# Input projections of a delta-rule stage taken by pairs of channel tiles in seven block products, with operands parked in DRAM

## The chip, the cores and the metric

One core of one Trainium2 chip runs the whole kernel. The metric is device microseconds of one execution, the median of several runs. TensorE multiplies, VectorE, ScalarE and GpSimd work elementwise, and the SyncE queue issues all DMAs.

## What is computed

One decoder block over x of 1024 tokens by 1024 features, in float32. Cut to what matters here:

```python
proj = x @ w_in                       # columns: q k v z beta a | sparse attention | merge gates
q, k, v = silu(causal_dwconv4(q|k|v)) # 4 heads of 128, taps along the tokens
o_A  = chunk_gated_delta(l2norm(q), l2norm(k), v, g, beta)   # chunks of 64 tokens
o_A  = rmsnorm(o_A) * silu(z)
o_B  = native_sparse_attention(...)   # compressed, selected and window branches
m    = sigmoid(gA) * (o_A @ W_A) + sigmoid(gB) * (o_B @ W_B)
h    = LayerNorm(alpha * x + m @ W_out)
out  = LayerNorm(alpha * h + (silu(c_g) * c_v) @ W_down)     # [c_g|c_v] = dwconv3(h @ W_up)
```

## The kernel before

Products are made in three matmuls: each operand is split into a rounded part (`h`) and its residue (`l`), and `h*h`, `h*l`, `l*h` are added up. A weight tile of 1024 x 128 is loaded (`load_cols`, L186), rounded on ScalarE and its residue taken on GpSimd (`split`, L180 to L184). x is kept transposed in four SBUF blocks `xT` (rounded and residue, two halves of 512 tokens), from the pool `S6` of six buffers of 2 MB; the other two hold `vS` (attention values) and `gA` (gates and output of the delta rule).

The head (L244 to L273): for each of eight token tiles, `turn_x` transposes x on TensorE, ScalarE and VectorE write the two parts, and `v_group` makes the attention values with 24 matmuls of 288 columns. Behind it small constants are prepared: masks, `chan_cols` and `pos_cols` (L308 to L334; taps and position vectors, loaded into `st`, which has two buffers, and transposed), the decays `gg` and their running sums `gc`.

The delta-rule stage (L426 to L705) makes 33 projections, each `proj_gen` (L415): 48 matmuls of 512 columns into a two-bank PSUM tile `big` (two of them) and then a `use`: `act_gen` (convolution and silu of q, k, v, 12 tiles), `z_gen` (4), `mix_gen` (merge gates, 16 tiles, stored to DRAM) and, at the end, one key projection of the attention. `PLAN` (L39) says which are made in which of nine units. Into their matmuls two generators are woven for each of 4 heads x 2 halves: `pre` (L477: norms, decay matrices, inversion of the unit lower triangular matrix, its 16 x 16 blocks by a loop of small VectorE operations L534 to L550 with DRAM images in between) and `scan` (L616: the state recurrence over four pairs of chunks). `PRE` and `SCAN` (L35, L36) say at which part of a unit each step of theirs is issued. TensorE's order is the order in which the program issues (`manual_schedule`, for TensorE alone); the other engines and SyncE are ordered by the scheduler of the language. PSUM has eight banks: two `big` of two, and four `sm` of one.

After the stage the attention, the merge and the feed-forward part follow. The feed-forward products of `W_up` are made in seven block products already, in an order that a planner of the kernel works out.

Of the kernel before, what the change touches and what calls it, by code (L numbers as in the profile page):

```python
# [16 lines left out]
OP = mybir.AluOpType  # L17
# [21 lines left out]
def PLAN(z, M, QKV, F):  # L39
    return [[F(z, 1)] + M(3), QKV(1) + M(1), [F(z, 2)] + M(2), QKV(2) + M(1),  # L40
            [F(z, 3)] + M(2), QKV(3), M(3), M(3), M(1)]
# [105 lines left out]
def hybrid_block_kernel(ctx: ExitStack, tc: tile.TileContext, x, w_in, gdn_conv_w, gdn_a_log,  # L147
# [16 lines left out]
    psb = ps_cm.enter_context(tc.tile_pool(name="psb", bufs=2, space=bass.MemoryType.PSUM))  # L164
    pss = ps_cm.enter_context(tc.tile_pool(name="pss", bufs=4, space=bass.MemoryType.PSUM))
    dram = ctx.enter_context(tc.tile_pool(name="dram", bufs=1, space=bass.MemoryType.DRAM))

    def big():
        return psb.tile([128, 1024], F32, name="big", tag="big")

# [29 lines left out]
    xT = {}  # L200
    for hf in range(2):
        for p in "hl":
            xT[p, hf] = S6.tile([128, KT, 512], F32R, name=f"xT{p}{hf}", tag="s")
# [9 lines left out]
    ones = const.tile([128, 128], F32, name="ones")  # L213
    V.memset(ones, 1.0)
# [8 lines left out]
    sp = gmask.tile([128, NT, 32], F32, name="sp")  # L223
# [17 lines left out]
    for tt in range(2, NT):  # L241
        load_x(tt)

    def turn_x(tt):  # L244
        ps = big()
        for k in range(KT):
# [3 lines left out]
        A.activation(xT["h", hf][:, :, o:o + 128], psv, AF.Copy)  # L250
        V.tensor_tensor(xT["l", hf][:, :, o:o + 128], psv,
                        xT["h", hf][:, :, o:o + 128].bitcast(F32), op=OP.subtract)
# [14 lines left out]

    with tc.manual_schedule(engines=MS):
        turn_x(0)
        for tt in range(NT):  # L270
            if tt + 1 < NT:
                turn_x(tt + 1)
            v_group(tt)  # L273
    triu = gmask.tile([128, 128], F32, name="triu")
# [15 lines left out]
    eye = gmask.tile([32, 16, 16], F32, name="eye")  # L290
    V.memset(eye, 0.0)
    for i in range(16):
        V.memset(eye[:, i, i:i + 1], 1.0)
# [14 lines left out]
    def chan_cols(src, taps, tiles, name):  # L308
        st = xin.tile([128, 1024], F32, name="st", tag="st", bufs=2)[:tiles, :taps * 128].rearrange("p (k c) -> p k c", k=taps)
# [117 lines left out]
    with gd as gp:  # L427
# [49 lines left out]
        def pre(h, hf, st):  # L477
# [108 lines left out]
            for b in (16, 32, 64):  # L586
# [10 lines left out]
                if b < 64:  # L597
                    X = g5("X")
# [1254 lines left out]
```

## Time and profile before

| | us |
|---|---|
| median of 3 runs | 1719.05 (1718.46 to 1721.38) |
| profiled execution, its own time | 1719.78 |
| its span, first to last instruction | 1718.0 |
| TensorE busy | 1675.0 |
| VectorE, GpSimd, ScalarE busy | 1116.2, 788.1, 734.2 |

The page of the profile gives the busy time of each engine and the chain of work that ended last, followed back from the end. The views below it give windows of time, single instructions in order of time, groups of instructions by line, and waits. A TensorE instruction's listed duration includes its pipeline, so its cost in a stream is read from start to start.

### The profile page before, as it was taken

What the parts mean: (1) busy time and instruction counts of PE and PEld (TensorE: products, weight loads), DVE (VectorE), ACT (ScalarE), POOL (GpSimd) and SP (SyncE); (2) the same over time, 40 slices, a digit from 0 to 9 for tenths busy, and PEclk for the clock granted to TensorE, in tenths of its full rate; (3) what the DMA queues carried; (4) which work ended last, traced back from release to release, by engine and by line L of the source; (5) the groups of instructions that cost most, each with busy time, mean ns of one, the idle gap of its engine ahead of it and who ended that gap; (6) DMA issues with size and microseconds to landing.
All of it is one profiled execution on the core that took longest, in us unless ns stands there. A gap on an engine that the chain in (4) does not pass through costs nothing.

```text
span 1718.0 us, 23466 instructions
## 1 busy us (share of the span) xinstructions
PE 1675.0 (97%) x8562; PEld 1411.7 (82%) x8562; DVE 1116.2 (65%) x2089; ACT 734.2 (43%) x1269; POOL 788.1 (46%) x640
## 2 busy tenths in 40 slices
PE   8999999999999998999999999999999999999997
PEld 8888888888888877888877887788888888888885
DVE  3545647657433358899874328988677667865656
ACT  3422323223222458788843115544444444443333
POOL 1322222232212537887657236678877777210005
PEclk9999999999999999999999999999999999999998
DMA  5222121221221312334125612333332232687722
GB/s 177 75 63 76 56 66 45 61 75 33 87 81 52 98 63 96 126 105 132 35 87 184 224 58 89 111 107 116 118 104 93 98 112 98 215 315 269 234 88 98
DMA packets 199024, 189.88 MB, mean 111 GB/s; under 512 B 19656, under 2 KB 155005, under 8 KB 198909
## 3 DMA queue, kind: packets, MB, share of 16 engines
q1 hardware_dynamic: 198909, 188.39, 34.3%
q8 instruction: 67, 1.10, 0.3%
q14 instruction: 48, 0.39, 0.1%
HBM read 136.97 MB, written 51.38 MB: 110 GB/s over the span
## 4 chain that ended last, share of the span: by engine, by line
PE 82%; DVE 7%; issue 3%; ACT 3%; POOL 3%; DMA 2%; SPq 0%; ACTq 0%; POOLq 0%; DVEq 0%
PE pq L193 37%; PE big L193 29%; PE sm L193 12%; PE sm L983 2%; DVE st L917 1%; ACT P L919 1%; POOL P L872 1%; DVE wh L991 1%; DMA w<-in_w_out_dram 1%; DVE wl L991 1%; DVE st L881 0%; DVE wb L1454 0%; DMA w<-in_w_down_dram 0%; DMA wsum<-w 0%; PE big L247 0%
## 5 line engine op out<-in xcount | busy, mean ns | idle before, releaser
L183 POOL TENSOR_TENSOR wl<-w,wh 128x1024 fp32r<-128x1024 f32 (+2 forms) x51 | 123.1, 2418 | 362.1 <-PE big L193 132.9
L193 PE MATMUL big<-xTl,wh 128*128 128x512 f32 x608 | 244.1, 402 | 0.0
L193 PE MATMUL big<-xTh,wh 128*128 128x512 f32 x608 | 244.1, 401 | 0.0
L193 PE MATMUL pq<-wd 128*128 128x512 f32 x924 | 209.6, 389 | 0.0
L193 PEld LDWEIGHTS pq<-wd 128*128 128x128 f32 x924 | 173.4, 188 | 36.0
L193 PE MATMUL pq<-xb,wb 128*128 128x512 f32 x792 | 187.6, 391 | 2.0 <-DVE accs L1465 1.5
L1465 DVE SCALAR_TENSOR_TENSOR accs<-pq,fcw,accs 128x510 f32<-128x510 f32 (+3 forms) x264 | 144.5, 568 | 61.0 <-ACT accs L1553 56.1
L193 PEld LDWEIGHTS pq<-xb,wb 128*128 128x128 f32 x792 | 148.5, 188 | 34.8 <-issue 2.8
L193 PE MATMUL big<-xTh,wl 128*128 128x512 f32 x608 | 160.3, 399 | 0.0
L193 PEld LDWEIGHTS big<-xTl,wh 128*128 128x128 f32 x608 | 114.7, 189 | 20.7 <-issue 0.2
L193 PEld LDWEIGHTS big<-xTh,wh 128*128 128x128 f32 x608 | 114.7, 189 | 20.6
L193 PE MATMUL pq<-mTh,wb 128*128 128x512 f32 x528 | 127.6, 397 | 3.2 <-ACT mTh L1253 3.1
L193 PEld LDWEIGHTS big<-xTh,wl 128*128 128x128 f32 x608 | 110.9, 188 | 21.4
L193 PE MATMUL pq<-mTl,wb 128*128 128x512 f32 x528 | 127.3, 391 | 0.0
L872 POOL TENSOR_TENSOR P<-P,st 128x640 f32<-128x640 f32 (+6 forms) x94 | 106.3, 1160 | 45.1 <-DVE st L881 19.7
L193 PEld LDWEIGHTS pq<-mTh,wb 128*128 128x128 f32 x528 | 101.1, 192 | 25.8 <-ACT mTh L1253 3.3
L193 PEld LDWEIGHTS pq<-mTl,wb 128*128 128x128 f32 x528 | 99.1, 188 | 21.2
L1454 POOL TENSOR_TENSOR wb<-w,wb 128x512 fp32r<-128x512 f32 x79 | 103.7, 1319 | 27.2 <-ACT wb L1253 27.2
L182 ACT ACTIVATE wh<-w 128x1024 fp32r<-128x1024 f32 (+2 forms) x51 | 53.1, 1046 | 134.8 <-PE big L193 90.7
L193 PE MATMUL big<-kS,qS 128*128 128x320 f32 (+5 forms) x384 | 86.7, 343 | 3.2 <-ACT P L919 2.0
L919 ACT ACTIVATE P<-big,st 128x640 f32<-128x640 f32 (+6 forms) x112 | 83.3, 749 | 10.3 <-DVE st L917 9.5
L1253 ACT ACTIVATE wb<-w 128x512 fp32r<-128x512 f32 x85 | 53.3, 629 | 80.3 <-PE pq L193 76.0
(394 smaller groups left out, 3558.1 us busy)
## 6 DMA issues: line engine op xcount, KB each, us to landing
w<-in_w_in_dram SPq DMA_DIRECT2D x40, 512.0 KB, 3.9
w<-in_w_up_dram SPq DMA_DIRECT2D x36, 512.0 KB, 3.8
w<-in_w_down_dram SPq DMA_DIRECT2D x53, 256.0 KB, 3.7
wsum<-w SPq DMA_DIRECT2D x44, 256.0 KB, 2.5
sig<-th SPq DMA_DIRECT2D x32, 256.0 KB, 2.2
w<-sig SPq DMA_DIRECT2D x30, 256.0 KB, 3.3
wx<-in_w_up_dram SPq DMA_DIRECT2D x11, 512.0 KB, 3.8
gdrC<-accs SPq DMA_DIRECT2D x11, 512.0 KB, 2.6
```

The costliest lines, as they stand in the source:

```text
L182: A.activation(wh[:, :n], w[:, :n], AF.Copy)
L183: G.tensor_tensor(wl[:, :n], w[:, :n], wh[:, :n].bitcast(F32), op=OP.subtract)
L193: PE.matmul(o, a, b, start=start, stop=stop, skip_group_check=True)
L872: G.tensor_tensor(p, p, r.to_broadcast([128, p.shape[1]]), op=OP.mult)
L917: V.reduce_max(nm, pv if m > 1 else pv[:, 0], axis=AX.X, negate=True)
L919: A.activation(P[:, r0 + i, :n], pv[:, i], AF.Exp, bias=nm[:, i:i + 1], accum_out=su[:, i:i + 1])
L983: PE.transpose(tp[:n, r * 128:(r + 1) * 128], P[:, r, c0:c0 + n], ident)
L991: V.tensor_tensor(pl, tp[:n], ph.bitcast(F32), op=OP.subtract)
L1253: A.activation(o, i, AF.Copy)
L1454: e.tensor_tensor(H.tile[:, 1], src(), H.tile[:, 0].bitcast(F32), op=OP.subtract)
L1465: V.scalar_tensor_tensor(o, i, fcw[:, 2 - s, j:j + 1], o, op0=OP.mult, op1=OP.add)
```

## The change

The 32 projections of the delta-rule stage are taken by pairs of channel tiles. For a pair, the weights are 2 x 2 blocks (two channel tiles by two halves of the features), x has 2 x 2 blocks (two halves of the features by two halves of the tokens), and the four results come from seven block products of 12 matmuls (the scheme of Strassen and Winograd) with sums of blocks before and after. The sums of x are made once: on GpSimd from the rows of x (`row_sums`), turned on TensorE (`turn_sum`), as blocks 6, 7, 4 and 5. The sums of the weights are made on GpSimd for each pair. The results are combined by VectorE in four PSUM banks of one each (`psbk`, in place of the two `big`), and each `use` is now called by halves of the tokens.

To make room, `vS` and one block of x are stored to DRAM in the head and loaded again at the end of the stage; z and the gated output go to DRAM tiles `zd` and `gAd`, and `gA` is loaded at the end. The row of running decay sums is stored to DRAM (`gcd`) and read back by every `pre` as a broadcast, in place of a product with `triu`. `chan_cols` and `pos_cols` move into the hand-ordered head, behind value group 4. In `pre`, the two scalings of `kt` move from GpSimd to ScalarE, the unit matrix in `XB` is made on GpSimd, and the turn of v comes later; several tiles have fewer buffers. One plan over nine units replaces `PLAN`: one pair is made ahead, then the matmuls of the others are spread evenly.

```diff
-PRE = [0.0, 0.04, 0.07, 0.1, 0.14, 0.2] + [0.72 + 0.05 * i for i in range(8)]
-SCAN = [1.13 + 0.085 * i for i in range(8)] + [1.81, 1.86, 1.92]
+PRE = [0.0, 0.07, 0.1, 0.14, 0.8] + [0.82 + 0.05 * i for i in range(8)]
+SCAN = [1.2 + 0.085 * i for i in range(8)] + [1.88, 1.93, 1.99]
+PAIRS = ["kq0", "vz0", "m", "kq1", "vz1", "m", "kq2", "vz2", "m", "m", "kq3", "vz3", "m", "m", "m", "m"]
+SPAN = 9.0
...
+    XS = {1: XK[0, 0], 2: XK[1, 0], 3: XK[1, 1], 6: xblock("xT2"), 7: xblock("xT3", S7)}
+    def row_sums(tt):
+        (a, b), (c, d) = [[xi[t][:, hs] for hs in HS] for t in (tt - 4, tt)]
+        rows = {5: a, 6: d, 7: c, 4: b}
+        for o, x, y in ((a, c, a), (c, d, c), (d, d, a), (b, d, b)):
+            G.tensor_tensor(o, x, y, op=OP.subtract)
+        return rows
+    def turn_sum(n, tt, row):
+        ps = sm()
+        for k in range(4):
+            PE.transpose(ps[:, k * 128:(k + 1) * 128], row[:, k * 128:(k + 1) * 128], ident)
...
+        A.activation(r[:, 0], psv, AF.Copy)
+        V.tensor_tensor(r[:, 1], psv, r[:, 0].bitcast(F32), op=OP.subtract)
...
             v_group(tt)
+            if tt % 2:
+                nc.sync.dma_start(vsp[:, (tt - 1) * 512:(tt + 1) * 512],
+                                  vS[:, tt - 1:tt + 1].rearrange("p t b s d -> p (t b s d)").bitcast(F32))
+            if tt == 4:
...
+                gcw = chan_cols(gdn_conv_w[0], 4, 12, "gcw")
+                fcw = chan_cols(ffn_conv_w[0], 3, 2 * NFF, "fcw")
+                nrw = chan_cols(gdn_norm_w, 1, 1, "nrw")
...
+                peT = {"k": pos_cols(cmp_pos_k, "pek"), "v": pos_cols(cmp_pos_v, "pev")}
+            if tt >= 4:
+                rows[tt] = row_sums(tt)
+            if tt == NT - 1:
+                nc.sync.dma_start(xsp, XK[0, 1].rearrange("p i k c -> p (i k c)").bitcast(F32))
+            for t in {5: (4,), 6: (5,), 7: (6, 7)}.get(tt, ()):
+                for n in (6, 7):
+                    turn_sum(n, t, rows[t][n])
+        for n, name in ((4, "xT4"), (5, "xT1")):
+            XS[n] = xblock(name)
+            for t in range(4, NT):
+                turn_sum(n, t, rows[t][n])
...
+            gr = g5("tmp", 3)
+            nc.sync.dma_start(gr, bass.AP(tensor=gcd.tensor, offset=gcd.offset + (hf * 16 + h) * 128,
+                                          ap=[[0, 128], [512, 4], [1, 128]]))
             yield
-            gb = g5("tmp", 3)
-            A.activation(gb, gg[:, cs, h, None].to_broadcast([128, 4, 128]), AF.Copy)
-            gr = sm()
-            for c in range(4):
-                mm(gr[:, csl[c]], gb[:, c, :], triu)
             dS = g5("tmp", 3)
...
-            G.tensor_tensor(kb, kt, bc(nb), op=OP.mult)
-            G.tensor_tensor(kd, kd, bc(egd[:, cs, h]), op=OP.mult)
+            for c in range(4):
+                A.activation(kb[:, c], kt[:, c], AF.Copy, scale=nb[:, c:c + 1])
+                A.activation(kd[:, c], kd[:, c], AF.Copy, scale=egd[:, hf * 4 + c, h:h + 1])
...
+        PORD = (1, 6, 2, 7, 5, 4, 3)
+        class Seven:
+            def make(self):
...
+                sub = functools.partial(G.tensor_tensor, op=OP.subtract)
+                if n == 1:
+                    self.load(2 * g + 1)
+                    src = A11
+                elif n == 6:
+                    self.load(2 * g + 2)
+                    G.tensor_tensor(self.s, A21, A22, op=OP.add)
+                    sub(A21, A11, A21)
+                    sub(A11, self.s, A11)
+                    src = A11
...
+                t = self.ring[self.made % 5]
+                A.activation(t[:, :512], src, AF.Copy)
+                sub(t[:, 512:], src, t[:, :512].bitcast(F32))
...
+            def steps(self):
+                u2, u3 = self.uu[:, HS[0]], self.uu[:, HS[1]]
+                for _ in range(4):
+                    self.make()
+                for g, ((_, one), (_, two)) in enumerate(self.pairs):
+                    a, b, c, d = (self.banks[i] for i in ((0, 2, 1, 3) if g % 2 else range(4)))
+                    bank = {1: a, 2: a, 6: b, 4: b, 7: c, 5: d, 3: d}
+                    for n in PORD:
+                        self.make()
...
+                        if n == 1:
+                            A.activation(u2, a, AF.Copy)
+                        elif n == 6:
+                            V.tensor_tensor(u2, b, u2, op=OP.add)
+                        elif n == 7:
+                            V.tensor_tensor(u3, c, u2, op=OP.add)
+                        elif n == 5:
+                            V.tensor_tensor(c, d, u3, op=OP.add)
+                            two(1, c)
+                        elif n == 2:
+                            one(0, a)
+                        elif n == 4:
+                            V.tensor_tensor(b, u3, b, op=OP.subtract)
+                            two(0, b)
+                        else:
+                            V.tensor_tensor(d, d, u2, op=OP.add)
+                            one(1, d)
...
+                XK[0, 1] = xblock("xK01b")
+                nc.sync.dma_start(XK[0, 1].rearrange("p i k c -> p (i k c)").bitcast(F32), xsp)
+                yield from proj_gen(C_KC, kc_ps.append, one_bank)
...
+            fg, done = chain(), 0
+            for _ in range(84):
+                next(fg)
+            for x, _, g in ev:
+                while done < x * (84 * len(PAIRS) - 84 + 48) / SPAN:
+                    next(fg, None)
+                    done += 1
+                next(g, None)
...
+    vS = S6.tile([128, NT, 2, 4, 64], F32R, name="vS", tag="s")
+    nc.sync.dma_start(vS.rearrange("p t b s d -> p (t b s d)").bitcast(F32), vsp)
+    gA = S6.tile([128, 4, T], F32, name="gA", tag="s")
+    for j in range(4):
+        nc.sync.dma_start(gA[:, j], gAd[j])
```

## Rows read from the trace of the kernel before

**Rows 1.** The page: shares of the span by engine in the chain.
```profile
PE 82%; DVE 7%; issue 3%; ACT 3%; POOL 3%; DMA 2%; SPq 0%; ACTq 0%; POOLq 0%; DVEq 0%
```
**Rows 2.** Windows: window, length, busy PE, PEld, DVE, ACT, POOL, granted clock, DMA.
```profile
20.00:40.00 20.00, 20.00 (x160) 20.00 (x159) 8.88 (x16) 7.14 (x11) 0.00 (x0) 1.00 0.30 82
...
1200.00:1300.00 100.00, 100.00 (x440) 82.37 (x439) 69.75 (x115) 43.47 (x72) 80.20 (x62) 1.00 0.32 106
...
44.00:545.00 501.00, 499.89 (x2738) 427.43 (x2738) 274.63 (x740) 143.87 (x240) 127.45 (x76) 1.00 0.23 64
```
**Rows 3.** The chain in order of time: start, length, what, merged.
```profile
534.20 8.49 PE big L193 x37
...
1115.99 590.20 PE pq L193 x2592
```
**Rows 4.** Timeline of TensorE: start, duration, instruction; head, stage start, decay product, end.
```profile
36.66 1.03 PE L247 MATMUL big<-ident,x 128*128 128x128 f32 x8
37.45 0.38 PE L193 MATMUL sm<-wh,xTh 128*128 128x288 f32 x1
...
45.08 0.51 PE L193 MATMUL big<-xTh,wh 128*128 128x512 f32 x1
...
146.59 1.05 PE L193 MATMUL sm<-triu,tmp 128*128 128x128 f32 x8
147.40 0.48 PE L193 MATMUL big<-xTh,wh 128*128 128x512 f32 x1
...
545.95 0.39 PE L193 MATMUL sm<-xTh,wh 128*128 128x512 f32 x1
```
**Rows 5.** Timeline of TensorE behind two idle waits (in brackets, with the releaser).
```profile
684.31 0.62 PE L983 MATMUL sm<-ident,Pc 128*64 128x128 f32 x4 [2.28 <-DVE oB L968]
...
1067.41 9.02 PE L193 MATMUL pq<-mTh,wb 128*128 128x512 f32 x24 [3.09 <-ACT mTh L1253]
```
**Rows 6.** Windows of 4 us behind these waits: busy PE, granted clock, DMA.
```profile
684.00:688.00 4.00, 3.69 (x17) 0.59 0.55 169
...
1068.00:1072.00 4.00, 3.88 (x10) 0.50 0.03 9
```
**Rows 7.** DMA issues: count, size, median us from issue to landing.
```profile
w<-in_w_in_dram SPq DMA_DIRECT2D x40, 512.0 KB, 3.9
...
hres<-h SPq DMA_DIRECT2D x8, 512.0 KB, 2.6
...
AB<-aimg SPq DMA_DIRECT2D x8, 32.0 KB, 1.9
```
**Rows 8.** Groups of instructions by form: count, busy us, mean ns, idle before.
```profile
L1454 POOL TENSOR_TENSOR wb<-w,wb 128x512 fp32r<-128x512 f32 x79 | 103.7, 1319 | 27.2 <-ACT wb L1253 27.2
...
L1614 POOL TENSOR_TENSOR accs<-accs 128x512 f32<-128x512 f32 x13 | 22.1, 1700 | 47.6 <-ACT wd L1701 34.7 <-DVE accs L1614 12.8
...
L389 POOL TENSOR_TENSOR rr<-ss,mhalf 128x4 f32<-128x4 f32 x16 | 16.1, 1008 | 6.9 <-DVE ss L493 6.4
...
L1253 ACT ACTIVATE wb<-w 128x512 fp32r<-128x512 f32 x85 | 53.3, 629 | 80.3 <-PE pq L193 76.0 <-DMA w<-in_w_up_dram 2.6 <-issue 1.0
...
L881 DVE TENSOR_TENSOR st<-st,gates 128x4 f32<-128x4 f32 x48 | 21.3, 443 | 0.9
L1570 DVE TENSOR_TENSOR u<-pq,u 128x512 f32<-128x512 f32 x22 | 15.1, 685 | 0.9 <-PE pq L193 0.2
```
**Rows 9.** Timeline of GpSimd and VectorE in the delta-rule stage.
```profile
187.55 2.38 POOL L183 TENSOR_TENSOR wl<-w,wh 128x1024 fp32r<-128x1024 f32 x1 [11.29 <-ACT tmp L648]
...
187.88 2.08 DVE L651 TENSOR_TENSOR ms<-ms,sc 128x4 f32<-128x4 f32 x1
...
193.19 0.12 DVE L654 TENSOR_TENSOR ms<-ms,rr 128x4 f32<-128x4 f32 x1
```
**Rows 10.** Window of the operations on tile `pr`: busy VectorE.
```profile
60.00:530.00 470.00, 53.86 (x256) 1.00 0.23 65
```
**Rows 11.** Waits: engine, line, waited for, total us, times, longest.
```profile
POOL ms L389 <- DVE ms L652: 30.3, 8, 11.5
```

More of the change, by code (lines that the diff above doesn't have):

```diff
@@ L169, in big, with one_bank @@
         return psb.tile([128, 1024], F32, name="big", tag="big")
+    def one_bank():
+        return psb.tile([128, 512], F32, name="bk", tag="bk")
     def sm():
@@ L198, in hybrid_block_kernel, with xblock, __init__, __getitem__ @@
     V.tensor_copy(identr, ident)
[L200 to L203, printed above, removed]
+    def xblock(name, pool=S6):
+        return pool.tile([128, 2, 4, 512], F32R, name=name, tag="s")
+    XK = {(kh, hf): xblock(f"xK{kh}{hf}") for hf in range(2) for kh in range(2)}
+    class Blocks:
+        def __init__(self, p, hf):
+            self.p, self.hf = "hl".index(p), hf
+        def __getitem__(self, i):
+            return XK[i[1] // 4, self.hf][i[0], self.p, i[1] % 4, i[2]]
+    xT = {(p, hf): Blocks(p, hf) for hf in range(2) for p in "hl"}
     def row_bcast(src, n, name, pool=const, tag=None):
@@ L242, in hybrid_block_kernel @@
         load_x(tt)
+    scr = xin.tile([128, 840], F32, name="scr")
+    sp = scr[:, 0:256].rearrange("p (t c) -> p t c", t=NT)
+    triu, ones = scr[:, 256:384], scr[:, 384:512]
+    gct = stream.tile([32, 128], F32, name="gct", tag="wl")
+    av, s0, s1, s2, s3, gg = (scr[:, 512 + 32 * i:544 + 32 * i].rearrange("p (t h) -> p t h", h=4) for i in range(6))
+    alog, dtb = scr[:, 832:836], scr[:, 836:840]
     def turn_x(tt):
@@ L376, in hybrid_block_kernel @@
     V.tensor_copy(gc, ps[:, 0:32].rearrange("p (t h) -> p t h", h=4))
+    ps = sm()
+    PE.transpose(ps[:32, :128], gc.rearrange("p t h -> p (t h)"), ident)
+    V.tensor_copy(gct, ps[:32, :128])
+    gcd = dram.tile([32, 128], F32, name="gcd")
+    nc.sync.dma_start(gcd, gct)
     ps = sm()
@@ L421, in hybrid_block_kernel @@
     xin_cm.close()
-    gA = S6.tile([128, 4, T], F32, name="gA", tag="s")
+    pb_cm.close()
+    psb = banks("psbk", 4)
+    gAd = [dram.tile([128, T], F32, name=f"gAd{j}") for j in range(4)]
+    zd = [dram.tile([128, T], F32, name=f"zd{j}") for j in range(4)]
     summed, held = list(range(2 * KD)), []
@@ L567, in pre @@
             yield
-            ps = sm()
-            for c in range(4):
-                PE.transpose(ps[:, csl[c]], vT[:, tsl[c]], ident)
-            vb = g5("vb")
-            V.tensor_tensor(vb, v4(ps), bc(bv), op=OP.mult)
-            yield
             qd = g5("qd")
@@ L657, in scan @@
             yield
+            zt = gp.tile([128, 512], F32, name="zt", tag="th", bufs=2)
+            nc.sync.dma_start(zt, zd[h][:, HS[hf]])
             yield
@@ L667, in hybrid_block_kernel, with pair_of @@
         mixes = iter(range(16))
[L669 to L673 removed]
+        PCOL = (C_GQ, C_GK, C_GV)
+        def pair_of(name):
+            if name == "m":
+                a, b = next(mixes), next(mixes)
+                return (C_MIX + a * 128, MixUse(a)), (C_MIX + b * 128, MixUse(b))
+            h = int(name[2])
+            if name[:2] == "kq":
+                return (C_GK + h * 128, ActUse(1, h)), (C_GQ + h * 128, ActUse(0, h))
+            return (C_GV + h * 128, ActUse(2, h)), (C_Z + h * 128, ZUse(h))
```

299 lines of the change are left out of this document (171 added, 128 removed).

## The prediction

> **What bounds the kernel now.** I read the page's busy times and its chain first: TensorE is busy 1675 of 1718 us and carries 82% of the chain [rows 1]. Then the stretch that the change touches, by windows. From the first input projection of the delta rule to the last before the attention stage, 45.1 to 546.0 us [rows 4], TensorE is busy 499.9 of 501 us, VectorE 274.6, ScalarE 143.9, GpSimd 127.5 [rows 2]. "Busy" may hide stalls, so I took the pitch of the projection matmuls: 37 in 8.49 us (0.229 us each) here, 2592 in 590.2 us (0.228) in the feed-forward part [rows 3]. 33 projections x 48 x 0.228 = 361 us; the other 140 us are the small matmuls of `pre` and `scan` woven in. So in this stage every TensorE instruction that goes is time won, and every wait of TensorE on anything is time lost. The change must be summed in those two columns.
>
> **TensorE work.** 32 projections of 48 matmuls become 16 pairs of 7 products of 12: 1536 becomes 1344, 192 fewer. 192 x 0.228 = **43.8 us less**. The product of the decay row with `triu` goes (it is read from DRAM instead): eight instructions from 146.59 to 147.40, 0.81 us a unit [rows 4], eight units, **6.5 us less**. Added are the turns of the four row sums of x for tiles 4 to 7: 64 transposes; eight take 0.79 us (36.66 to 37.45) [rows 4], so **6.3 us more**. Net **-44.0 us**. One extra small transpose (`gct`) and one event fewer a unit I take as nothing; at 0.1 us each they can't matter.
>
> **The head (up to the first product).** Before, the five small loads of `chan_cols` and `pos_cols` and their transposes lay outside the hand-ordered block and were slipped in where they fitted. Now they stand in TensorE's written order behind value group 4, and their staging tile `st` has two buffers for five loads. The third and the fourth load can start only when the first two have been transposed, the fifth only after the third: two DMA round trips in front of which TensorE stands. The smallest transfer with a time, 32 KB, lands in 1.9 us [rows 7]; with issue and hand-over I take 2.5 us each, **5.0 us**. The low end is 0 (if the scheduler puts other work there), the high end 2 x 3.9, a weight load's time [rows 7]. An idle wait of this size has a second price here: after waits of 2.28 and 3.09 us [rows 5] the granted clock read 0.59 and 0.50 in the next 4 us [rows 6], that is, partly or wholly the 1.2 GHz level, and 24 matmuls took 9.0 us instead of 5.5. I count one such drop, **3.4 us** (9.0 - 5.5), between none and two.
> Then the turns: after the last value group twelve of the sixteen still come, each read out of one of four PSUM buffers by ScalarE and VectorE (0.69 us [rows 8], against 0.4 us of TensorE), and the block `xT4` needs the buffer of `vS` or of one x block, which is free only when its store has landed (2.6 us for 512 KB [rows 7]; the x block is 2 MB, so about 10 us, begun some 5 us earlier). TensorE must wait until the four turns of that block are read. I take **4.0 us**, between 1 (VectorE's pace alone) and 8 (the 2 MB store ends last). The row sums themselves, 16 operations of 1.3 us on GpSimd [rows 8], lie in a stretch in which it does nothing today, 0 us from 20 to 40 [rows 2]; they cost nothing there. Head: **12.4 us**, bounds 1 and 23.
>
> **The steady part: feeding TensorE.** Per pair GpSimd now has 11 operations of 512 columns (four sums, seven residues) in place of two of 1024: 11 x 1.32 [rows 8] = 14.5 us per pair, against TensorE's (501 - 43.8 - 6.5 - 11 for the last projection) / 16 = 27.5 us. With 24 powers of 1.0 us it is about 57% busy. Weights are made four products (11 us) ahead. The feed-forward part runs the same seven products with GpSimd at 80% and VectorE at 70% and TensorE never idle [rows 2]; I cost the weights at nothing, and the cover is that lead. ScalarE gains copies and the two scalings of `kt`, roughly 60 us on 144, and stays under half.
> VectorE gains five combinations a pair, 80 x 0.69 = 55 us [rows 8], and 36 small end pieces of the convolution, 6 us (0.16 each, an estimate from the 0.12 us row [rows 9]); it loses 2 us of copies. 274.6 + 59 = 333 of about 451 us, 74%. On average that is room. In order it is less: product 3 adds onto the bank from which VectorE must first have taken product 5, and only product 4 (12 x 0.228 = 2.74 us) lies between. Less its own 0.69 us, VectorE may be 2.05 us late. Before, a finished projection had a second buffer and 11 us.
> What makes VectorE late is the small triangular inverse of each unit, 53.9 us in eight bursts of 6.7 us [rows 10]. And these bursts get longer: a VectorE operation with both inputs in SBUF waits while GpSimd works. At 187.88 one on 128x4 took 2.08 us and ended with GpSimd's 2.38 us operation begun at 187.55; its like at 193.19, with GpSimd free, took 0.12 us [rows 9]. In the attention stage, where GpSimd is busy most of the time, the mean of such an operation is 0.44 us [rows 8], 0.28 above what I take it to need. 16 of them in a burst add 4.5 us: 11.2 us. A product 5 ends in it with chance 11.2 / 27.5 = 0.4; the mean rest, 5.6 us, less 2.05 is 3.5 us; 8 x 0.4 x 3.5 = **11 us**. Bounds: 0 (the combinations are slipped between the small operations) and 40 (the third case below).
>
> **Moved data.** `vS`, one x block, the gates and the z tiles go to DRAM and back: some 16 MB more beside a DMA load of 23% [rows 2]. At the end of the stage the x block (2 MB) comes back while the last five products run, 13.7 us, and the last projection does not read it for another 16 matmuls, 3.7 us; the stores and loads at 2.6 to 3.9 us per 512 KB fit. The parked values are needed only in the attention stage. The two-buffer PSUM pool is opened again behind one projection (11 us); its first tile waits for the readers of the last projection, now in halves. I take **1 us**, 0 to 5. No part after that is changed; it only starts earlier.
>
> **Sum**, against the profiled execution (1718.0 us span, 1719.8 us its own time): 1719.8 - 44.0 + 12.4 + 11 + 1 = 1700.2. The median shown is 0.7 us under that execution: **1699.5 us**.
>
> **Rivals.**
> *All of it hidden.* TensorE's saving comes through and the waits fall into one another. For it: 501 us without 2 us of idle today, and the feed-forward part does the same at full pace [rows 2]. Against it: the loads in written order, which I see nothing to cover. 1719.8 - 44.0 + 2 - 0.7 = 1677.
> *GpSimd becomes the feed that is late.* If each residue waits for its ScalarE copy (7 x 0.63), the second weight tile's reload (3.9 us, issued only when its buffer's last reader is done) is bare in each pair, and the powers hold GpSimd as today (24 us busy and about 37 us waiting, 30.3 of it in one row [rows 11]: 3.8 a pair), a pair takes 14.5 + 4.4 + 3.9 + 3.8 = 26.6 us, just under 27.5. At 1.70 us an operation, which the one GpSimd row beside busy two-input VectorE work shows [rows 8], it is 30.8. Between (1.51 us): 28.7, 1.2 x 16 = 19 us: 1719.8 - 44.0 + 12.4 + 1 + 11 + 19 - 0.7 = 1718.5, no change.
> *Slower: VectorE becomes the bound through GpSimd.* It has 30 operations with two SBUF inputs a unit: the 16, five on 128x4, one on q, and the eight decay operations, whose source the change moves from PSUM to SBUF. If each of 240 waits half a GpSimd operation, 0.66 us, VectorE needs 333 + 158 = 491 us against TensorE's 451: 1719.8 - 44.0 + 12.4 + 1 + 40 - 0.7 = 1728.5. It decides from a mean wait of 0.62 us on: (481 - 333) / 240, where 481 is the length that eats the gain. Against it: the measured 0.28 us of a stage where GpSimd is as busy. The Trainium skill, "SBUF — State Buffer", section "SBUF: two separate sides", states it as a lock: one of the two engines fully blocks for the other's whole instruction, also for a VectorE instruction with two SBUF inputs beside a GpSimd one that reads SBUF. By that rule the 0.66 is what a random meeting costs, and the time would be this case's; the 2.08 us row agrees with the lock, the 0.44 us mean says that most don't meet.
>
> **Chances.** Forecast, 1686 to 1712: 0.55. All hidden, 1676 to 1686: 0.24. GpSimd late, around 1718: 0.10 (0.04 still faster, 0.06 within). VectorE bound: 0.11 (0.10 slower, 0.01 within). A measurement of this kernel can tell about 0.2% (3.4 us) from no change. Faster 0.55 + 0.24 + 0.04 = 0.83, same 0.07, slower 0.10. The range leaves out the slower case and the edges: 1677 to 1718.
>
> **What would show it.** Of after: 84 product matmuls a pair at 0.229 us; `triu` by `tmp` gone. In the head, two gaps of TensorE before the transposes of `st` and one before the first product; the first product at about 45.1 + 6.3 + 12.4 = 64 us. TensorE's waits in the steady part name VectorE at products 3, in the bursts of `pr`. Wrong would be: waits named GpSimd (the feed), a GpSimd mean above 1.4 us, VectorE over 90% busy from 65 to 510 us, or no gap at `st`.

## The result, and the profile after

The changed kernel takes 1739.1 us (median of four runs, 1737.8 to 1739.7) against 1719.9 us before (four runs, 1718.5 to 1721.4): a ratio of 1.0111, 95% interval 1.0095 to 1.0126. It is slower, by 19 us. The forecast was 1699.5 us, with a range up to 1718; the sign was wrong and so was the range.

The first thing to look at is again the chain of what ended last. Before, TensorE carried 82% of it [rows 1]; after:

```profile
PE 63%; DVE 17%; DMA 7%; POOL 5%; issue 4%; ACT 4%; SPq 0%; POOLq 0%; ACTq 0%; DVEq 0%
```

VectorE's share went from 7% to 17%, that of transfers from 2% to 7%. So TensorE now waits. The windows say where: first the whole stage of the delta rule (first product to the end of its last projection), then its beginning and the rest. Columns as in [rows 2]: window, length, busy PE, PEld, DVE, ACT, POOL, granted clock, DMA share, GB/s.

```profile
52.71:547.40 494.69, 460.49 (x2468) 384.40 (x2467) 359.02 (x852) 202.71 (x409) 261.55 (x216) 0.98 0.31 94
...
53.00:100.00 47.00, 37.20 (x172) 29.48 (x171) 35.78 (x78) 26.51 (x53) 24.10 (x22) 0.89 0.19 55
...
100.00:547.40 447.40, 423.00 (x2295) 354.64 (x2294) 322.95 (x775) 175.91 (x357) 237.16 (x195) 0.99 0.33 98
```

The same stretch before:

```profile
45.08:534.60 489.52, 488.41 (x2683) 418.00 (x2683) 271.73 (x731) 140.57 (x237) 125.39 (x74) 1.00 0.23 65
```

TensorE has 215 matmuls fewer, but is idle for 34.2 us (494.69 - 460.49) instead of 1.1. One correction to my reading of before: the 501 us that I took for the stage [rows 2, 4] held one projection of the attention stage (11 us); by its own work the stage was 489.5 us.

Who it waits for (waits of TensorE in the stage: line waited for, us in total, times, longest):

```profile
PE sm L199 <- DVE Z L666: 8.5, 9, 3.5
PE sm L199 <- DVE Y L661: 5.8, 6, 1.6
PE sm L199 <- DVE S L706: 4.8, 1, 4.8
PE sm L627 <- DVE sil L543: 4.6, 1, 4.6
PE sm L199 <- ACT kc L682: 2.7, 3, 1.1
PE bk L199 <- ACT uu L831: 2.7, 1, 2.7
```

They name VectorE, as forecast, but at other places: not product 3 and its bank (`bk`), but the woven steps of the inverse and of the scan (`Z`, `Y`, `S`), which lie only some 7 product matmuls apart.

The ledger of the profiled executions (span 1737.8 against 1718.0 us, +19.8): TensorE's work -44.0, which is the forecast's sum and not a measurement, though the counts came as forecast. Up to 100 us: the first product starts 7.6 us later (52.71, before 45.08), then come 9.8 us idle and 4.1 us lost to the lower clock (half of the 8.2 us that TensorE is busy there, rows below), less 2.8 for the 28 turns ahead of the first product, which are in the -44.0 already: +18.7. From 100 us to the end of the stage +38.1 (what is left over): 23.4 us more idle, 4.7 us of lower clock, and some 10 us by which TensorE's own busy time is longer than the counts say. The attention part is 2.6 us longer, the feed-forward part 4.2, the end 0.2. So against a saving of 44 us, 57 us were lost in the head and in the stage, and 7 us behind it.

What such a wait looks like from inside (timeline: start, duration, engine, line, operation; idle before in brackets):

```profile
243.49 1.28 POOL L789 TENSOR_TENSOR ws<-w 128x512 f32<-128x512 f32 x1 [2.98 <-DMA w<-in_w_in_dram]
...
243.86 5.03 DVE L580 SCALAR_TENSOR_TENSOR tmp<-tmp,gc,mdt 128x128 f32<-128x128 f32 x4
...
244.84 1.28 POOL L790 TENSOR_TENSOR w<-w 128x512 f32<-128x512 f32 x1
...
246.08 1.31 POOL L807 TENSOR_TENSOR wl<-w,wl 128x512 fp32r<-128x512 f32 x1
...
247.47 1.26 POOL L791 TENSOR_TENSOR w<-ws,w 128x512 f32<-128x512 f32 x1
248.81 0.68 DVE L666 TENSOR_TENSOR Z<-sm,Z 128x512 f32<-128x512 f32 x1
...
249.54 2.08 PE L199 MATMUL sm<-Z,tmp 128*128 128x128 f32 x8 [3.50 <-DVE Z L666]
```

Four decay operations of VectorE, 0.34 us each before, when their source lay in PSUM (a row of before further down), take 5.03 us together, as long as the four GpSimd operations beside them: each of the four stands still for one of those. `Z` stands behind them, and TensorE behind `Z`, 3.50 us. Then the granted clock is at its lower level, as in three other stretches of the stage:

```profile
67.90:74.70 6.80, 5.14 (x12) 4.08 (x13) 0.89 (x2) 1.98 (x6) 5.04 (x4) 0.50 0.45 118
95.20:98.60 3.40, 3.07 (x10) 2.59 (x11) 3.40 (x12) 1.39 (x3) 0.00 (x0) 0.50 0.02 5
248.80:255.60 6.80, 6.06 (x19) 5.27 (x20) 5.39 (x14) 6.36 (x17) 1.44 (x2) 0.50 0.00 0
474.10:477.50 3.40, 3.40 (x10) 2.90 (x11) 3.33 (x7) 1.24 (x3) 0.00 (x0) 0.50 0.00 0
```

### The profile page after: what moved, and what is told of

It is laid out like the page before. It is cut to its first block, busy times and chain, and to the rows that moved or that the text cites. A ratio compares the mean times of both kernels' runs of the same rounds, so it can differ in the third digit from the quotient of the medians.

```text
span 1737.8 us, 23772 instructions
## 1 busy us (share of the span) xinstructions
PE 1656.3 (95%) x8371; PEld 1382.7 (80%) x8371; DVE 1208.0 (70%) x2213; ACT 798.5 (46%) x1453; POOL 947.0 (54%) x800
## 4 chain that ended last, share of the span: by engine, by line
PE 63%; DVE 17%; DMA 7%; POOL 5%; issue 4%; ACT 4%; SPq 0%; POOLq 0%; ACTq 0%; DVEq 0%
PE pq L199 34%; PE big L199 9%; PE bk L199 9%; PE sm L199 8%; PE sm L1164 2%; DMA tmp<-gcd 2%; DVE sil L530 1%; DVE st L1098 1%; DVE Y L606 1%; POOL P L1053 1%; ACT P L1100 1%; DMA w<-in_w_in_dram 1%; DVE wh L1172 1%; DVE tmp L575 1%; DMA Z<-zimg 1%
## 5 line engine op out<-in xcount | busy, mean ns | idle before, releaser
L199 PE MATMUL bk<-xT,wh 128*128 128x512 f32 x456 | 125.6, 412 | 0.5 <-DVE sil L543 0.5
L807 POOL TENSOR_TENSOR wh<-w,wh 128x512 fp32r<-128x512 f32 x59 | 76.6, 1301 | 67.3 <-PE bk L199 40.9
L199 PE MATMUL bk<-xK,wh 128*128 128x512 f32 x384 | 106.5, 412 | 2.7 <-ACT uu L831 2.7
L199 PEld LDWEIGHTS bk<-xT,wh 128*128 128x128 f32 x456 | 84.7, 194 | 16.8 <-DVE sil L543 0.7
L443 POOL TENSOR_TENSOR sb<-sb,mhalf 128x1 f32<-128x1 f32 x8 | 4.3, 549 | 171.6 <-DVE sb L1951 171.6
L1098 DVE TENSOR_REDUCE st<-big 128x1 f32<-128x640 f32 (+7 forms) x88 | 83.4, 947 | 5.8 <-PE big L199 5.8
L1734 ACT ACTIVATE accs<-pq,fcw 128x512 f32<-128x512 f32 x88 | 59.0, 685 | 58.8 <-PE pq L199 22.2
L199 PE MATMUL bk<-xT,wl 128*128 128x512 f32 x312 | 86.0, 409 | 0.0
```

Source lines behind the costliest of these rows:

```text
L199: PE.matmul(o, a, b, start=start, stop=stop, skip_group_check=True)
L807: sub(t[:, 512:], src, t[:, :512].bitcast(F32))
L1098: V.reduce_max(nm, pv if m > 1 else pv[:, 0], axis=AX.X, negate=True)
L1734: return P.add("A", .58, lambda _: A.activation(acc(i)[:, HS[h]], t[bank], AF.Copy, scale=fcw[:, 2, j:j + 1]), deps, take=list(take))
```

## The experiments

The theories: *lock* (VectorE's operations with two SBUF inputs stand still while a GpSimd operation runs, and what is behind them in VectorE's order comes late), *load* (VectorE's five combinations a pair are simply too much), *row* (VectorE stands in order behind the decay row's load from DRAM), and *feed* (GpSimd's own results, the weights and the powers of the norms, are late). Medians, ratio to before with its 95% interval, and the length of the feed-forward part:

| run | median us | ratio | feed-forward us |
|---|---|---|---|
| after | 1739.1 | 1.0111 [1.0095, 1.0126] | 594.4 |
| e1_row_tensor | 1738.1 | 1.0102 [1.0084, 1.0120] | 597.2 |
| e2_stale_residues | 1717.9 | 0.9984 [0.9966, 1.0001] | 594.4 |
| e3_no_combinations | 1738.5 | 1.0102 [1.0087, 1.0117] | 594.5 |
| e4_columns_outside | 1736.0 | 1.0088 [1.0073, 1.0103] | 594.4 |
| e5_before_idle_gpsimd | 1731.4 | 1.0073 [1.0055, 1.0091] | 590.2 |
| e6_products_first | 1736.9 | 1.0101 [1.0077, 1.0125] | 594.4 |
| e7_residues_vector | 1728.7 | 1.0051 [1.0032, 1.0070] | 594.5 |
| e8_shift_64 | 1739.4 | 1.0111 [1.0079, 1.0143] | 594.4 |
| e9_before_shift_32 | 1718.4 | 0.9990 [0.9974, 1.0006] | 590.2 |
| c1_all_relief | 1745.6 | 1.0156 [1.0128, 1.0183] | 594.4 |
| c2_less_order | 1731.0 | 1.0066 [1.0042, 1.0090] | 594.4 |
| e10_place | 1740.4 | 1.0125 [1.0106, 1.0143] | 595.2 |
| f4_row_tensor | 1736.1 | 1.0087 [1.0063, 1.0111] | 595.2 |
| f3_vector_residues | 1728.1 | 1.0053 [1.0035, 1.0071] | 595.2 |
| f2_vector_and_row | 1743.5 | 1.0137 [1.0105, 1.0169] | 595.2 |
| g2_small_on_gpsimd | 1738.2 | 1.0115 [1.0098, 1.0132] | 594.4 |
| g1_vector_residues_small | 1725.5 | 1.0037 [1.0024, 1.0050] | 595.2 |

**GpSimd's residues taken away (e2).**
```diff
-                sub(t[:, 512:], src, t[:, :512].bitcast(F32))
+                if self.made < 5:
+                    sub(t[:, 512:], src, t[:, :512].bitcast(F32))
```


> The seven residue subtractions of a pair are made for the first five products only and then left out, so that GpSimd has 4 operations of 512 columns a pair instead of 11; the low halves of the later weights are stale, that part of the product is not computed rightly, but TensorE, VectorE and ScalarE do the same instructions. Theory LOCK: GpSimd's 145 us of residues in the stage go, VectorE's busy time from 60 to 548 us falls by about 20 us and TensorE's waits on Z, Y and S (19 us) mostly go with their half-clock stretches: 1739 - 20 to 30 = 1709 to 1719 us. Theory LOAD or ROW: VectorE's order is as full as before, no more than 5 us gained: 1734 to 1739 us. Weight feed too late (GpSimd itself): waits named GpSimd would go; there are hardly any, so 0 to 3 us.

1717.9 us: 21 us gained with nothing taken from TensorE, VectorE or ScalarE. Windows of the stage and TensorE's waits in it:

```profile
54.02:526.20 472.18, 453.50 (x2469) 381.25 (x2468) 323.76 (x851) 203.21 (x409) 121.86 (x109) 0.99 0.32 98
```
```profile
PE sm L199 <- DVE Z L666: 4.1, 5, 1.6
...
PE sm L199 <- DVE Y L661: 1.5, 4, 0.6
```

VectorE's busy time falls from 359 to 324 us with the same operations; TensorE's idle time from 34.2 to 18.7 us. That is inside lock's expectation; load and row allowed 5 us at most. Lock or feed: the waits that went had named VectorE, and VectorE's own waits on GpSimd's powers (`ms`, L724) are 5.7 us in all here and 4.4 after, so these did not shrink. Both speak for lock, but the run takes away the load of both.

**The same load on the kernel before (e5).** This one separates them, since nobody reads what the added operations write.
```diff
-        yield from chan_gen(ps, ws, xT)
+        for i, _ in enumerate(chan_gen(ps, ws, xT)):
+            if i in (8, 24, 40) and len(idle) < 99:
+                idle.append(G.tensor_tensor(spare[0], spare[0], spare[0], op=OP.subtract))
+            yield
```


> The kernel BEFORE, with 99 GpSimd operations of 512 columns (both inputs in SBUF) added to the stage, three in each of its 33 projections, that write a tile nobody else reads; the tanh tile has two buffers for three, to make room. Nothing waits for them, GpSimd's busy time in the stage goes from 125 to about 255 us as in the changed kernel; TensorE's work stays. Theory LOCK: VectorE's busy time in the stage rises by 20 to 35 us with no operation added to it, TensorE gets waits on Z, Y and S, though fewer than after since VectorE has no combinations: 1722 to 1735 us. Theory FEED (what counts is GpSimd's own results coming late: weights and powers): the powers come about 1 us later, weights are a whole projection ahead: 1720 to 1722 us, VectorE's busy time unchanged.

1731.4 us, 11 us slower than before, 9.6 of them in the stage. Window of its stage, then the added operations and operations of VectorE by form (count, busy us, mean ns, idle before):

```profile
45.00:545.00 500.00, 492.31 (x2688) 419.67 (x2687) 302.04 (x729) 139.41 (x236) 231.29 (x175) 1.00 0.23 64
```
```profile
L422 POOL TENSOR_TENSOR dum<-dum 128x512 f32<-128x512 f32 x99 | 107.7, 1088 | 6.0
```
```profile
L471 DVE SCALAR_TENSOR_TENSOR sil<-th,sil 128x512 f32<-128x512 f32 x24 | 22.8, 952 | 14.5 <-ACT th L470 14.2
...
L520 DVE SCALAR_TENSOR_TENSOR tmp<-sm,gc,mdt 128x128 f32<-128x128 f32 x32 | 9.0, 341 | 0.0
...
L501 DVE TENSOR_SCALAR ss<-ss 128x4 f32<-128x4 f32 x8 | 2.8, 355 | 0.0
L550 DVE TENSOR_REDUCE XB<-pr 32x7 f32<-32x49 f32 x16 | 2.4, 186 | 0.0
```

The same four forms before (their line numbers are eight lower):

```profile
L463 DVE SCALAR_TENSOR_TENSOR sil<-th,sil 128x512 f32<-128x512 f32 x24 | 16.6, 690 | 17.1 <-ACT th L462 16.9
L512 DVE SCALAR_TENSOR_TENSOR tmp<-sm,gc,mdt 128x128 f32<-128x128 f32 x32 | 9.2, 342 | 0.0
...
L542 DVE TENSOR_REDUCE XB<-pr 32x7 f32<-32x49 f32 x16 | 2.4, 186 | 0.0
L493 DVE TENSOR_SCALAR ss<-ss 128x4 f32<-128x4 f32 x8 | 1.3, 161 | 0.0
```

VectorE's busy time in the stage rises from 272 to 302 us with no operation added to it, and by kind: two SBUF inputs, 690 to 952 ns; one PSUM and one SBUF input, 342 to 341; reduction, 186 to 186; but also an operation with one SBUF input on 128x4, 161 to 355. The Trainium skill, "SBUF — State Buffer", section "Who interferes with whom", names these: two SBUF inputs against a GpSimd instruction that reads SBUF, and `tensor_scalar` where it runs in a two-port mode, while reductions never contend. The rows here agree with all three, though no run shows in which mode the 128x4 operation ran.

TensorE's waits in this stage (before, only `Z` was there, 1.0 us in two waits):

```profile
PE sm L193 <- DVE S L644: 2.3, 1, 2.3
PE sm L193 <- DVE pev L331: 2.0, 1, 2.0
PE sm L193 <- DVE Z L604: 1.2, 2, 0.7
PE sm L193 <- DVE S L646: 1.0, 1, 1.0
PE big L193 <- DVE gA L453: 0.8, 1, 0.8
```

None names GpSimd, and VectorE's waits on the powers are 1.1 us as before. Lock holds, and feed isn't needed for it. One thing more differs from before: to make room, the tanh tile has two buffers for three. That lengthens no operation of VectorE, but the wait on `gA` may come from it.

**VectorE's load taken away (e3).** The five `V.tensor_tensor` combinations in `steps` are deleted.


> The five VectorE combinations of a pair are left out (the users read the banks as the products left them; what is computed is no longer the projection): 80 operations, 55 us of VectorE. Theory LOAD: TensorE's waits on VectorE go with their half-clock stretches, 1739 - 25 to 35 = 1704 to 1714 us. Theory LOCK: the bursts are as long as they were, the combinations were 16% of VectorE's time, a sixth to a third of the waits goes: 1729 to 1735 us. Theory ROW: 1733 to 1739 us.

1738.5 us, nothing gained, and the waits stay:

```profile
PE sm L199 <- DVE Z L666: 7.7, 6, 3.4
PE sm L199 <- DVE Y L661: 4.8, 5, 1.6
PE sm L199 <- DVE S L706: 3.9, 1, 3.9
```

Fifty-five microseconds of VectorE on PSUM sources cost nothing, while 35 us of standing still cost 21. Load falls. The gain is smaller than lock's own expectation (1729 to 1735) too: the combinations are hardly a part of what makes `Z` late.

**The residues on VectorE (e7).** `sub(t[:, 512:], ...)` becomes `V.tensor_tensor(t[:, 512:], ..., op=OP.subtract)`.


> The seven residue subtractions of a pair move from GpSimd to VectorE; nothing is left out. VectorE gets 112 operations of 512 columns, some 0.68 us each, 76 us. Theory LOCK: what it loses to waiting goes (the run without residues had 36 us less of VectorE time), the net load is 352 - 36 + 76 = 392 of about 475 us, 83%, and as the combinations (55 us) cost nothing in their run, the time is near that of the run without residues: 1715 to 1728 us. Theory LOAD: 83% in order brings back more waits than it saves: 1740 to 1760 us.

1728.7 us, just above lock's expectation (load's began at 1740), and half of what leaving them out gains. VectorE then works 388 us of 488 in the stage, and is still better off than with 359 us in GpSimd's company.

**The decay row (e1, f4).** The lines of the kernel before come back (`gb`, `mm(gr[:, csl[c]], gb[:, c, :], triu)`); the room for `triu` comes from other constants, in e1 those that later parts use, in f4 the gates.


> One part undone: the decay row comes from TensorE again (eight instructions a unit, gg times triu into a PSUM tile) instead of from DRAM; to make room the identity for the attention masks and the feed-forward convolution weights are put back behind the stage. Theory LOCK (VectorE's operations with two SBUF inputs stand still while GpSimd works, and everything behind them on VectorE comes late): the 64 decay operations go back to one SBUF input, their mean from 0.45 to about 0.34 us (7 us of VectorE), TensorE pays 6.5 us for the product; the two cancel, 1736 to 1745 us. Theory ROW (VectorE stands in order behind the row's load, 8.9 us in six waits, and this is what makes it late): the stage becomes at least 15 us shorter in spite of the product, 1715 to 1725 us. Theory LOAD (the five combinations a pair alone are too much): 1739 + 6.5 = 1745 us.

1738.1 us, inside lock's expectation: row falls as the main cause. But the stage itself is 489.3 us instead of 494.7 in spite of 6.5 us more for TensorE; the later parts give it back (feed-forward 597.2 us). f4 avoids that, and is compared with e10, which has the same places:


> The kernel of the run above with the decay row from TensorE again; the room for triu comes from the gates, which wait in DRAM during the stage. If VectorE's wait for the row's load (8.9 us) and the decay operations' second SBUF input (7 us) cost what the first run of that kind had in its stage (12 us saved, 6.5 us of TensorE paid), 4 to 7 us less than the run above; if the gain was only moved to later parts, as that run's total said, 0.

1736.1 against 1740.4 us: 4.4 us less, inside what was expected, though the two intervals still touch. If it holds, the way through DRAM saves TensorE 6.5 us and costs about 11, for two things together that f4 does not separate: the second SBUF input of the decay operations, and VectorE's wait for the load (in the changed kernel; us in total, times, longest):

```profile
DVE tmp L575 <- DMA tmp<-gcd: 8.9, 6, 1.9
```

**The head (e4, e6).** e4 puts `chan_cols` and `pos_cols` back behind the ordered block. e6 puts the first two products ahead of the gate chain.


> One part undone: the five small column loads and their transposes stand outside the hand-ordered block again, behind the turns. If the two gaps of TensorE at these transposes and the half clock behind them are the price of the written order, the end of value group 7 comes 5 us earlier and the kernel 3 to 5 us: 1734 to 1736 us. If that time is only moved (the turns and the first product wait for VectorE and for the store of the x block anyway, the columns then stand before the first product): 1737 to 1741 us.

> The changed kernel with the first two products (and their copy u2) ahead of the gate and decay chain, in the order of every engine. If product 2's wait on the copy (2.66 us), the waits beside it and the half clock from 67.9 to 74.8 us come from the copy standing behind the gate chain in ScalarE's order, the first 50 us of the stage become 6 to 10 us shorter: 1729 to 1733 us. If the gate chain is what the first unit waits for anyway, it only moves: the gap comes in front of the transposes of kt or the first decay row, 1736 to 1740 us.

e4 gains 3.1 us, at the edge of its first expectation; its interval and that of after overlap. The gaps that it removes are these of the changed kernel (timeline of TensorE):

```profile
34.65 0.19 PE L328 MATMUL sm<-ident,st 1*128 1x1 f32 x1 [1.06 <-DVE fcw L1396]
35.50 0.22 PE L343 MATMUL sm<-ident,st 32*128 32x32 f32 x1 [0.67 <-DMA st<-in_cmp_pos_k_dram]
36.63 0.21 PE L343 MATMUL sm<-ident,st 32*128 32x32 f32 x1 [0.91 <-DMA st<-in_cmp_pos_v_dram]
```

e6 gains 2.2 us, and its interval includes no gain: the wait on `uu` shrinks from 2.7 to 1.7 us, and the one on `sil` grows from 4.6 to 6.3. This points to VectorE's order, and not to where the products stand, as the limit of the head, but does not show it.

**Place (e8, e9, e10).** The feed-forward part, whose code is unchanged, is 4.2 us longer after. e8 and e9 shift all tiles behind the constants by 64 bytes down and 32 up; e10 shifts the weight tiles against the x blocks:
```diff
-                nrw = chan_cols(gdn_norm_w, 1, 1, "nrw")
-                nwh = const.tile([128, 1], F32, name="nwh")
+                nrw = chan_cols(gdn_norm_w, 1, 1, "nrw", small)
+                nwh = small.tile([128, 1], F32, name="nwh", tag="nwh", bufs=1)
```


> The changed kernel with two small constants (nrw, nwh) moved from the constants' pool to the stage's own pool: no instruction changes, but every SBUF tile behind the constants lies 64 bytes lower, so that the weight tiles begin at a multiple of 128 bytes as they did before the change (they lay 64 bytes off). Theory PLACE (TensorE's pitch depends on where its operands lie): the feed-forward part goes back from 594.4 to 590.2 us and the stage's products, which took 2.80 us for twelve, gain up to 5 us: 1730 to 1735 us. Theory NOT PLACE (the longer feed-forward part comes from something else that changed, such as the order in which transfers run beside it): 594.4 us stays, 1738 to 1740 us.

> The kernel BEFORE with an unused constant of 32 bytes: no instruction changes, every tile behind the constants lies 32 bytes higher and is no longer aligned to 128 bytes (nor to 64). Theory PLACE: the feed-forward part goes from 590.2 to about 597 us, as in the run with the decay row from TensorE, whose tiles lay 32 bytes off, and the projections get slower too: 1726 to 1735 us. Theory NOT PLACE: 1719 to 1721 us.

> The changed kernel with the two small constants nrw and nwh in the small pool, which lies between the weight tiles and the x blocks: no instruction changes, the weight tiles lie 64 bytes lower, the x blocks and all behind them stay where they were. The distance from a weight tile to an x block is then 64 bytes off a multiple of 128, as in the kernel before and in that kernel with all tiles shifted (feed-forward part 590.2 us in both), and not a multiple of 128 as in the changed kernel and all its variants (594.4 us). Theory DISTANCE: feed-forward part 590.2 us, the stage's products go from 2.80 to 2.75 us for twelve; 1739 - 4 - 5 = 1729 to 1735 us. Otherwise 594.4 us, and 1737 to 1741 us.

The piece of the chain that is the feed-forward part (start, length), in the order after, e8, e9, e10, e1:

```profile
1131.40 594.43 PE pq L199 x2592
```
```profile
1134.89 594.40 PE pq L199 x2592
```
```profile
1113.10 590.22 PE pq L194 x2592
```
```profile
1135.65 595.20 PE pq L199 x2592
```
```profile
1130.14 597.21 PE pq L199 x2592
```

My rule of the distance falls: e10 should have gone back to 590.2. What holds is that the length comes in a few fixed values (ten kernels with 594.4 or 594.5, five with 595.2, three with 590.2, each within 0.1 us), that a common shift does nothing, and that a shift of 64 bytes of the weight tiles alone moves it by 0.8 us. So part of TensorE's pitch hangs on places; that the 4.2 us do is likely, by which rule is open.

**Versions that might beat both (c1, c2, f3, f2, g2, g1).** c2 is e7 with e4, e6 and e8; c1 adds another order within a unit:
```diff
-PRE = [0.0, 0.07, 0.1, 0.14, 0.8] + ...
+PRE = [0.0, 0.12, 0.3, 0.36, 0.8] + ...
             Z = g5("Z")
             nc.sync.dma_start(Z, full_image(zi))
-            X = g5("X", 1)
-            V.transpose(X..., Z...)
 ...
+            X = g5("X", 1)
+            V.transpose(X..., Z...)
             vT = acts[2, h]
```


> The changed kernel with what the runs so far point to: residues on VectorE, column loads outside the ordered block, the first two products ahead of the gate chain, tiles shifted by 64 bytes, and in addition the decay row later (0.12 for 0.07), q's part at 0.30 and 0.36 instead of 0.10 and 0.14, and the transposition of Z into X put behind the wait-free part of a unit so that VectorE does not stand 24 us behind Z's reload. Sum: 1739 - 10.4 (residues) - 3 (columns) - 2 (products first) - 4 to 9 (place) - 5 to 12 (q's 7.4 us wait, Z's reload) = 1703 to 1715 us, faster than both. If VectorE at over 80% is late wherever the order is changed, nothing of the last term comes: 1715 to 1722 us.

> The same without the change of order inside a unit (decay row, q's part and the transposition of Z where the change has them). The difference from the run above is the price of VectorE standing in order behind q's part and Z's reload: 5 to 12 us if it is real, 1712 to 1722 us here; under 3 us if the waits only move.

1745.6 and 1731.0 us, both above all that was expected: the reliefs do not add up, and the order that was to free VectorE costs 15 us. In c1 TensorE waits 9.8 and 9.5 us for `sil` and 8.1 for the reload of `Z`, each once; the waits came in larger pieces elsewhere.

f3 is e10 with the residues on VectorE from the third pair on (`(G if g < 2 else V).tensor_tensor(...)`) and the columns outside; f2 adds the row from TensorE.


> The kernel of e10_place with the residues on GpSimd for the first two pairs only (VectorE is full there, GpSimd is not) and on VectorE from the third on, and the column loads outside the ordered block. By the runs of each: 10 us less for the residues and 3 for the columns, and up to 5 more since the first pairs no longer wait for VectorE: e10_place less 12 to 18 us; 1713 to 1722 us. If the head takes back what the columns give, less 8 to 11.

> Both: f3_vector_residues with the decay row from TensorE. With GpSimd's residues gone, little is left of the lock on the decay operations, but VectorE's wait for the row's load stays in the other run (9 to 10 us in all). If that wait is on the path: 2 to 5 us less than f3_vector_residues. If TensorE's 6.5 us are all that counts then: 4 to 7 us more.

1728.1 and 1743.5 us. f3 gains its 12 us; taking the row from TensorE, which gained 4.4 with the residues on GpSimd, loses 15 with them on VectorE, twice the most that was expected. In f2's profile TensorE waits 10.9 us for `Z`'s reload and 9.5 for `sil`, as in c1; what ties these two together I did not find.

g2 and g1 move the 128x4 operations from VectorE to GpSimd, with the residues on GpSimd and, in g1, as in f3 (`V.tensor_scalar(ss...)`, `V.tensor_tensor(bv...)` and so on become `G.`).


> The changed kernel with the 88 operations of 128x4 behind the norms of k, q and the output (11 a unit, 30.5 us of VectorE) on GpSimd, between the powers that are there already; two of them are written as two, 13 a unit. Theory LOCK: VectorE loses 30 us and the two hand-overs around each power go; 1739 - 8 to 15 = 1724 to 1731 us. Theory ORDER (GpSimd, now at over 60%, makes them later than VectorE did, behind residues of 1.3 us each): 1740 to 1750 us, with waits of TensorE on Am or S through GpSimd's small tiles.

> f3_vector_residues with the same operations on GpSimd, which has little else from the third pair on. VectorE at over 80% loses 18 us and GpSimd's order is nearly empty: f3_vector_residues (1728) less 5 to 12 us, 1716 to 1723 us, level with the kernel before. If VectorE's in-order waits on Z's reload and on PSUM are what is left, 1726 to 1729 us.

1738.2 and 1725.5 us: no gain with the residues on GpSimd (neither theory expected that), and 2.6 us with most of them gone, less than expected and inside the intervals. The tiny operations are victims (30.5 us in 88 operations after, 17.8 in e2). At 441.30 us of the changed kernel one of them (`ms`, L724) takes 1.26 us beside a residue, `Z` comes behind it, and TensorE waits 0.79 us for `Z`. How much of TensorE's waiting comes through them the two runs do not show, since on GpSimd these operations stand in GpSimd's order. g1 is the best full version, 0.37% above before: none of them beats it.

## Why the prediction was wrong, point by point

- **TensorE's saving, -44.0 us.** The count came: 1344 matmuls for 1536, `triu` gone, 64 turns. But some 10 us came back as longer busy time at the full clock. Some 3 of them are the pitch: the mean distance of two product starts in the stage is 232.2 ns, before 229.9. The rest I did not take apart.
- **The head, 12.4 us.** Measured 18.7 up to 100 us, inside the bounds. The two gaps came as three, 2.6 us for 5.0, and one drop of the clock. What I had wrong is the rest: the first product did not wait for the turns (52.71 us, not 64), but the waits behind it, on `uu` and `sil`, and two more stretches of half clock took more than that.
- **"I cost the weights at nothing, and the cover is that lead."** This is the step that failed. The lead covered the weights' arrival, and no wait of TensorE in the stage names GpSimd. It does not cover what the eleven operations do to VectorE while they run: the seven residues alone cost 21 us (e2). My proof was the feed-forward part, where GpSimd is as busy and TensorE never idle [rows 2]. There most of VectorE's work reads PSUM:

```profile
L1646 DVE SCALAR_TENSOR_TENSOR accs<-pq,fcw,accs 128x510 f32<-128x510 f32 (+3 forms) x264 | 144.6, 569 | 61.7 <-ACT accs L1734 54.1
```

  Operations with one input in PSUM were not lengthened by idle GpSimd work (342 and 341 ns in e5). Those with two SBUF inputs were held there too (24 additions of 512 columns, L1614 of the kernel before, took 1021 ns in the mean from 1200 us on), but TensorE did not have to wait for them. The cover came from a stage with fewer victims, and with none at a place where TensorE waits.
- **The steady part, 11 us.** Measured 38.1, near the upper bound of 40. VectorE's own work was forecast well: 333 us, and 324 in e2. The lock was in the sum, and its amount was about right: eight bursts of the small inverse with 4.5 us more each, 36 us; the residues cost VectorE 35 us (359 less 324). That the two agree is luck, since only some 12 of the 35 lie in the inverse. What the sum had wrong is the price: it was looked for at product 3, where 2 us of slack lie. The steps of the inverse and the scan, which alternate between TensorE and VectorE with about 7 matmuls between them, were never asked how late VectorE may be there. e2 gives back 21 of the 39.6 us between forecast and measurement; 6 more lie behind the stage, and what is left, in the head and the stage, the runs do not settle. The stage's length was misread too: with 489.5 us for 501 a pair has 26.8 us of TensorE, not 27.5, and the stage 439, not 451.
- **The decay row.** Its product counted as 6.5 us saved; that the row's load would stand in VectorE's order (8.9 us) was not costed at all, and that its source moves from PSUM to SBUF only in the rival. Net about 4 us lost (f4 against e10), not clear of the noise.
- **The combinations, 55 us of VectorE.** Rightly harmless on average, and harmless altogether (e3).
- **Moved data, 1 us.** The attention part is 2.6 us longer; within its bounds.
- **Nothing for the feed-forward part.** 4.2 us that no step of the sum could hold; likely the tiles' places, not shown.
- **The slower rival, chance 0.10.** Its mechanism is what happened, its condition is not, and its time, 1728.5 us, is 10.6 too short. It wanted VectorE full (a mean wait of 0.62 us over 240 operations); measured, VectorE stood still beside the residues for 35 us (359 less 324 in e2, where the sums of the weights still run), 0.15 us over the 240, and was 73% busy. The loss does not need a full VectorE. It needs one burst, such as the 5.03 us above, in front of one operation that TensorE waits for, and the half clock behind it. I priced a latency as a throughput, and so gave it 0.10.
- **The signs named.** Waits on VectorE, and gaps at `st`: right. "GpSimd mean above 1.4 us" and "VectorE over 90% busy" as what would show me wrong: neither came, and I was wrong all the same. GpSimd's mean is no sign of a lock in which VectorE is the one that waits.

The Trainium skill, "SBUF — State Buffer", section "SBUF: two separate sides", had the rule that I weighed and set low: full blocking for the other's whole instruction. The 5.03 us row agrees with it to the instruction.

Open: with the residues gone (e2) the stage is still 472 us, where the sum without losses wants about 440. Of these 32 us 18.7 are idle, mostly in the head and behind VectorE; the other 13 lie in TensorE's busy time and are explained in part only. And the two versions in which waits of 8 to 10 us appear at single places (c1, f2).

## What to carry to other kernels

Before work is put on an idle GpSimd, list what VectorE does beside it by operand: here those that read PSUM and reductions kept their times, those with two SBUF inputs and tiny scalar ones waited for whole GpSimd instructions. Then ask not how full VectorE is, but how late it may be at the tightest place where TensorE takes something back from it; a stage that runs well with the same busy shares is no proof unless its operands lie in the same memories and its results are wanted as soon. Removing an operation by fetching its result from DRAM puts a load into the order of the engine that reads it, and that wait belongs into the sum.

## What was not expected of the hardware

- A GpSimd operation that nobody waits for has a price: 99 of them (108 us) made VectorE 30 us busier and the kernel before 11 us slower (e5).
- An operation with a single SBUF input on 128x4 (`tensor_scalar`) is also held: 161 ns before, 355 beside the idle GpSimd work.
- The pitch of matmuls is not one number. In the first part of the feed-forward stage the mean distance of two starts was 228.0 ns before, 230.6 after, 231.2 in e10 and 232.3 in e1, and 226.7 in its last part before and after, with no wait between them.
- Behind a wait of 3.5 us the clock was at its lower level, 1.2 GHz, for 6.8 us (granted 0.50 from 248.8 to 255.6 us), and half of the 6.1 us in which TensorE was busy there is lost again; in the stage after, 20 us were spent so, in the stage before none.
